# Index scores by pairs of heads on the two halves of TensorE's rows

## The chip, the cores and the metric

The kernel runs on one core of a Trainium2 chip. The metric is the time of one execution in microseconds (us) on the device; the kernel before took 3161.13 us in the median of three runs (3159.14 to 3167.12).

## What is computed

One layer of a streaming encoder: 2048 tokens of width 1024, float32. The part that the change touches is the indexer of a sparse attention. For each block of 128 queries, eight index heads of 64 dimensions score all admissible keys:

```
rel       = relu(einsum('bqhd,bsd->bqhs', q_idx, k_idx) * 64 ** -0.5)
idx_score = einsum('bqh,bqhs->bqs', w_idx * 8 ** -0.5, rel)
sel       = top_k(idx_score, 256)        # the keys that attention may use
```

Before and after it stand one wide input projection, a pooling mixer, gates, the attention over the selected keys, an output projection, a layer norm, a gated MLP with a short convolution, and a second layer norm.

## The kernel before, in words

Products keep float32 accuracy by splitting an operand into a high part that the engine's fast float32 format (F32R) holds exactly and a low rest. `mm3` makes three products: high by high, high by low, low by high.

Tokens go in 4 groups of 512 (`G`) or 16 blocks of 128. The index keys have 64 dimensions, half of the array's 128 rows. `keys` transposes them doubled and writes `kst`: rows 0 to 63 hold the high part, rows 64 to 127 the low part. In `index_scores`, `double` copies each head's 64 query columns twice, `prepare` transposes the eight doubled heads into a PSUM tile and splits it, so two products of 128 rows, query high and query low against `kst`, give all four partial products. ScalarE (ACT) then evicts the PSUM tile with a Relu and VectorE (DVE) multiplies by the head's weight and adds. Blocks 0 and 1 need no scores. A block of more than 1024 keys is done in two spans, each with a PSUM tile from the pool of two (`PS2`).

The scores and the selection after them are a background generator (`scores_and_selection`, for the groups 0 and 1, then 2, then 3). `select` finds each query's 256th largest score by 32 counting passes over the score tile's bits (threshold tile `F`), then for each block a scan, the mask, and its store to DRAM. The foreground is the projections and then attention. At each foreground step `turn` adds to a credit 0.75 (`RATE`) of the PE time that the planner's clocks (`Paced`) counted since the last, and takes background steps as long as the credit is positive and the planned backlog of DVE and ACT is under 3 us. A step is charged with its DVE or ACT work, whichever is larger. In attention, `load_mask(b)` runs the background to the end of block b if its selection is not yet there. The framework then lays out each engine's instructions in an order of its own, by when it expects inputs and buffers to be ready; an engine starts them in that order.

In the profile all operations have the line of the recording helper (L133), so tiles tell them apart: `kst` the index keys, `F` the thresholds, `msk` the masks in DRAM, `mx` the running minimum of an attention score row, `ident` the identity of transposes, `p` PSUM tiles, `b` and `m` tiles of the large and the middle pool (42 and 8 buffers).

Of the kernel before, what the change touches and what calls it, by code (L numbers as in the profile page):

```python
# [9 lines left out]
F32 = mybir.dt.float32  # L10
F32R = mybir.dt.float32r
# [3 lines left out]
AF = mybir.ActivationFunctionType  # L15
# [4 lines left out]
P = 128  # L20
# [30 lines left out]
NPRE = 2  # L51
PN = (1, 1, 1)
PG = (0,)
HD, HP = 3, 5
XAT = 0
SPC, SPN, SPG = 0, 1, 0
TLAG = 3
# [10 lines left out]
NFIRST = 1  # L68
FINE = "fine"
PAUSE = "pause"  # L70
GRAIN = 1
RATE = 0.75
CAP = 1.5
EARLY = 2
SWITCH = "A--"
# [24 lines left out]
class Paced:  # L100
# [5 lines left out]
    def __getattr__(self, name):  # L106
        f = getattr(self._e, name)
        if not callable(f) or name == "dma_start":
            return f

        def call(*args, **kw):
            out = args[0] if args else kw["out"]
            n = out.free_size()
            if self._w == "pe":
                self._c.pe += 0.109 if name == "transpose" else 0.002 + max(n, 64) / 2400.0
            else:
                rate = {"dve": 1.04, "act": 0.84, "pool": 2.2}[self._w]
# [228 lines left out]
class Kern:  # L346
# [83 lines left out]
    def turn(self, step=None):  # L430
        for t in self.late:
            t[0] -= 1
        while self.late and self.late[0][0] <= 0:
            self.late.pop(0)[1]()
        if step != FINE:
            for dst, src in self.older:
                self.nc.sync.dma_start(dst, src)
            self.older, self.stores = self.stores, []
        pe, work = self.clocks.pe, self.clocks.work
        self.credit = min(self.credit + RATE * (pe - self.seen), CAP)  # L440
        self.seen = pe
        while self.bg and self.clocks.backlog() < SLACK and self.credit > 0:
            ready, gen = self.bg[0]
            if not ready():
                break
            before = dict(work)
            step = next(gen, "end")
            if step == "end":
                self.bg.pop(0)
            if step == PAUSE:  # L450
                break
            self.credit -= max(work["dve"] - before["dve"], work["act"] - before["act"])

    def run_to_end(self, gen):
        for step in gen:
# [47 lines left out]
    def setup(self):  # L503
# [6 lines left out]
        self.kst = self.keys_pool.tile([P, S], F32R, tag="kst", name="kst")  # L510
# [254 lines left out]
    def keys(self, g, krs, kds):  # L765
# [8 lines left out]
        nc.scalar.dma_start(self.d_kT[g], kT)  # L774
        self.keyed = g
        ks = slice(g * G, (g + 1) * G)
        nc.scalar.activation(self.kst[0:64, ks], pi[0:64], AF.Copy)
        kh = self.M([P, G], F32R)
        nc.scalar.activation(kh[64:128], pi[64:128], AF.Copy)
        nc.vector.tensor_tensor(self.kst[64:128, ks], pi[64:128], kh[64:128].bitcast(F32), op=OP.subtract)  # L780

    def head_values(self, g, rows):

# [221 lines left out]


    def index_scores(self, g):
        nc = self.nc
        blocks = [b for b in range(g * RB, (g + 1) * RB) if b >= 2]
        rows, doubled, parts = {}, {}, {}  # L1010
# [18 lines left out]
        for _ in range(PN[0] if g in PG else 1):  # L1029
            yield PAUSE  # L1030
        double(blocks[0])
        for _ in range(PN[1] if g in PG else 1):
            yield PAUSE
        prepare(blocks[0])
        for _ in range(PN[2] if g in PG else 1):
# [1 line left out]
        for b in blocks:  # L1037
            N = P * (b + 1)
            more = b + 1 in blocks
            if more:  # L1040
                load(b + 1)
            qh, ql = parts.pop(b)
            if N <= 1024:
                spans = [(0, N)]
            else:
                spans = [(0, N - SPLIT[b // 2]), (N - SPLIT[b // 2], N)]
            tiles = [self.T([P, hi - lo]) for lo, hi in spans]
            self.I[b] = tiles
            for h in range(IH):
                if h == HD and more:  # L1050
                    double(b + 1)
                if h == HP and more:
                    prepare(b + 1)
                wsc = self.ws[:, b, h:h + 1]
                for t, (lo, hi) in enumerate(spans):
                    nch = 1 if hi - lo <= 512 else 2
                    cw = (hi - lo) // nch
                    ps = self.PS2([P, 2, 512])
                    for c in range(nch):
                        ks = slice(lo + c * cw, lo + c * cw + cw)  # L1060
                        nc.tensor.matmul(ps[:, c, :cw], qh[:, h], self.kst[:, ks], start=True, stop=False)
                        nc.tensor.matmul(ps[:, c, :cw], ql[:, h], self.kst[:, ks], start=False, stop=True)
                    rl = self.T([P, nch, cw])
                    nc.scalar.activation(rl, ps[:, :nch, :cw], AF.Relu, scale=ID ** -0.5)
                    rl = rl.rearrange("p c w -> p (c w)")
                    if h == 0:
                        nc.vector.tensor_scalar(tiles[t], rl, wsc, None, op0=OP.mult)
                    else:
                        nc.vector.scalar_tensor_tensor(tiles[t], rl, wsc, tiles[t], op0=OP.mult, op1=OP.add)
                    yield  # L1070
            w = tiles[-1].shape[1]
            getattr(nc, MS).memset(tiles[-1][0:64, w - 64:w], NEG)

    def select(self, halves):

# [1048 lines left out]
```

## Time and profile before

| | |
|---|---|
| median of three runs | 3161.13 us |
| the profiled execution | 3160.95 us, span 3159.2 us |
| granted TensorE clock, mean | 0.989 |
| busy: PE, DVE, ACT, POOL | 96, 77, 51, 17% |
| instructions | 43928 |

Busy time of PE counts pipelined matmuls with modelled ends, so their starts say more than their lengths. PEld are PE's weight loads, one before each product. A row that ends in `[7.63 <-DVE mx]` was idle for 7.63 us until DVE wrote `mx`.

### The profile page before, as it was taken

To read this page: it belongs to the slowest core of one execution; us is meant where nothing else is said; L and a number is where in the kernel's file an instruction comes from. 1 tells how busy PE (TensorE), PEld (TensorE's weight loads), DVE (VectorE), ACT (ScalarE), POOL (GpSimd) and SP (SyncE) were. 2 spreads that over 40 slices of the span, in tenths; PEclk is the share of its full clock that TensorE was granted. 3 is DMA by queue.
4 is the path that set the end of the run, shared out by engine and by line. 5 is a ranking of instruction groups with operands and counts; after the bars stand their busy time and mean duration, and the time that the engine had idled before them with its cause. 6 is when DMAs were issued, how large, how long until landed. Compare 5 with 4: busy or idle time off the path is not lost. (4 is left out here: it accounts for less than half of the span.)

```text
span 3159.2 us, 43928 instructions
## 1 busy us (share of the span) xinstructions
PE 3041.4 (96%) x14750; PEld 2536.1 (80%) x14750; DVE 2445.5 (77%) x4563; ACT 1613.7 (51%) x3085; POOL 541.5 (17%) x528
## 2 busy tenths in 40 slices
PE   8999899999999999979999999999999999999998
PEld 8887688888888788768787778887778888888887
DVE  5588887987699899888776688999886655656676
ACT  3468846874578787657611144444442222433253
POOL 2002010010020221100231234554411111100011
PEclk9999899999999999989999999999999999999999
DMA  7668783755466332221264778887888866998753
GB/s 255 242 208 298 262 336 138 275 213 184 145 256 250 102 104 84 70 80 62 82 225 162 262 259 303 299 296 284 289 305 321 313 214 224 366 397 328 262 199 110
DMA packets 325872, 715.88 MB, mean 227 GB/s; under 512 B 27466, under 2 KB 132366, under 8 KB 325646
## 3 DMA queue, kind: packets, MB, share of 16 engines
q1 hardware_dynamic: 317006, 697.34, 62.0%
q10 hardware_dynamic: 8640, 15.73, 1.3%
q8 instruction: 117, 1.92, 0.3%
q14 instruction: 109, 0.89, 0.1%
HBM read 454.85 MB, written 258.11 MB: 226 GB/s over the span
## 5 line engine op out<-in xcount | busy, mean ns | idle before, releaser
L133 PE MATMUL p<-b,b 128*128 128x512 f32 (+3 forms) x12568 | 2824.0, 381 | 71.3 <-DVE b L133 25.9
L133 PEld LDWEIGHTS p<-b,b 128*128 128x128 f32 x12568 | 2255.5, 190 | 511.0 <-DVE b L133 32.9
L133 DVE TENSOR_TENSOR b<-p,b 128x512 f32<-128x512 f32 (+3 forms) x622 | 390.6, 654 | 144.6 <-PE p L133 97.8
L133 ACT ACTIVATE b<-p 128x512 fp32r<-128x512 f32 (+11 forms) x634 | 360.6, 604 | 259.1 <-PE p L133 244.0
L133 ACT ACTIVATE b<-b 128x512 fp32r<-128x512 f32 (+3 forms) x344 | 270.5, 805 | 323.2 <-DVE b L133 143.4
L133 DVE TENSOR_TENSOR b<-b,b 128x1024 fp32r<-128x1024 f32 (+6 forms) x302 | 340.0, 1136 | 87.5 <-ACT b L133 38.0
L133 ACT ACTIVATE m<-b,F 128x448 bf16<-128x448 f32 (+3 forms) x448 | 366.2, 820 | 52.8 <-DVE F L133 40.3
L133 DVE TENSOR_SCALAR_CACHE_REDUCE m<-b,F 128x512 bf16<-128x512 f32 (+6 forms) x476 | 372.5, 808 | 7.3 <-DMA gm<-m 3.8
L133 ACT ACTIVATE b<-m 128x512 fp32r<-128x512 f32 x215 | 133.3, 628 | 345.0 <-DVE m L133 133.7
L133 DVE SCALAR_TENSOR_TENSOR b<-b,cw,b 128x1023 f32<-128x1023 f32 (+1 forms) x176 | 246.2, 1411 | 69.7 <-ACT b L133 68.7
L133 ACT ACTIVATE b<-b,cw 128x1024 f32<-128x1024 f32 x88 | 106.9, 1236 | 269.5 <-DVE b L133 260.5
L133 POOL TENSOR_TENSOR b<-b,b 128x1024 f32<-128x1024 f32 (+3 forms) x62 | 148.8, 2402 | 490.2 <-DVE b L133 289.4
L133 PE MATMUL p<-ident,b 128*128 128x128 f32 x1248 | 199.0, 278 | 17.0 <-DVE b L133 8.9
L133 ACT ACTIVATE b<-b,mx 128x1024 f32<-128x1024 f32 (+2 forms) x192 | 171.6, 896 | 70.5 <-DVE mx L133 68.1
L133 PEld LDWEIGHTS p<-ident,b 128*128 128x128 f32 x1248 | 154.3, 142 | 53.1 <-DVE b L133 13.1
L133 DVE TENSOR_TENSOR b<-m,b 128x512 fp32r<-128x512 f32 x215 | 155.6, 732 | 53.1 <-ACT b L133 52.9
L133 DVE SCALAR_TENSOR_TENSOR b<-b,ws,b 128x768 f32<-128x768 f32 (+5 forms) x154 | 154.0, 1025 | 42.2 <-ACT b L133 39.3
L133 DVE CUSTOM_DVE_ANT_0 b<-p,b 128x1024 f32<-128x1024 f32 (+7 forms) x128 | 125.6, 984 | 39.1 <-PE p L133 30.9
L133 PE MATMUL p<-kst,b 128*128 128x384 f32 (+3 forms) x656 | 147.8, 358 | 2.8 <-ACT b L133 2.0
L133 ACT ACTIVATE m<-p 128x512 f32<-128x512 f32 (+2 forms) x172 | 100.8, 586 | 74.6 <-PE p L133 67.9
L133 PEld LDWEIGHTS p<-kst,b 128*128 128x128 f32 x656 | 111.0, 188 | 23.1 <-ACT b L133 12.4
L133 DVE TENSOR_TENSOR b<-p,m 128x512 f32<-128x512 f32 x132 | 89.7, 682 | 10.8 <-PE p L133 10.7
(126 smaller groups left out, 1528.4 us busy)
## 6 DMA issues: line engine op xcount, KB each, us to landing
b<-wk SPq DMA_DIRECT2D x339, 512.0 KB
wk<-b SPq DMA_DIRECT2D x211, 512.0 KB
b<-h SPq DMA_DIRECT2D x88, 512.0 KB
b<-in_w_ffn_up_dram SPq DMA_DIRECT2D x44, 512.0 KB
h<-b SPq DMA_DIRECT2D x44, 512.0 KB
b<-vv SPq DMA_DIRECT2D x80, 256.0 KB
hs<-b SPq DMA_DIRECT2D x33, 512.0 KB
b<-hs SPq DMA_DIRECT2D x33, 512.0 KB
```

The costliest lines, as they stand in the source:

```text
L133: return f(*args, **kw)
```

## The change

The keys are kept in two tiles, `kih` (high parts) and `kil` (low parts, a tile of the large pool for each 1024 keys), each with the same 64 dimensions on rows 0 to 63 and again on rows 64 to 127. The queries are transposed in pairs, head 2j on rows 0 to 63 and 2j+1 on rows 64 to 127, four transposes a block, and are not doubled. For each pair three products of 64 rows per head are written alternately for the two heads: query high by key high, query high by key low, query low by key high. Both PSUM tiles of the pool belong to one pair. A span that crosses key 1024 has its middle product in two pieces. The planner counts a 64-row product at half, and a scoring step (`LIGHT`) is charged with 0.75/0.95 of its work.

```diff
-HD, HP = 3, 5
+HP = 2
+LIGHT = "light"
+INDEX_RATE = 0.95
 # Paced
-                self._c.pe += 0.109 if name == "transpose" else 0.002 + max(n, 64) / 2400.0
+                half = name == "matmul" and args[1].shape[0] == ID
+                self._c.pe += 0.109 if name == "transpose" else (0.002 + max(n, 64) / 2400.0) / (2 if half else 1)
 # turn
-            self.credit -= max(work["dve"] - before["dve"], work["act"] - before["act"])
+            spent = max(work["dve"] - before["dve"], work["act"] - before["act"])
+            self.credit -= spent * (RATE / INDEX_RATE if step == LIGHT else 1.0)
 # keys
-        nc.scalar.activation(self.kst[0:64, ks], pi[0:64], AF.Copy)
-        kh = self.M([P, G], F32R)
-        nc.scalar.activation(kh[64:128], pi[64:128], AF.Copy)
-        nc.vector.tensor_tensor(self.kst[64:128, ks], pi[64:128], kh[64:128].bitcast(F32), op=OP.subtract)
+        if g % 2 == 0:
+            self.kil.append(self.T([P, 2 * G], F32R))
+        nc.scalar.activation(self.kih[:, ks], pi, AF.Copy)
+        nc.vector.tensor_tensor(self.kil[-1][:, (g % 2) * G:(g % 2 + 1) * G], pi, self.kih[:, ks].bitcast(F32), op=OP.subtract)
 # index_scores
-        def double(b):
-            qd = doubled[b] = self.T([P, IH, 2, ID])
-            nc.vector.tensor_copy(qd, rows.pop(b).rearrange("p (h d) -> p h d", d=ID)[:, :, None, :]
-                                  .to_broadcast([P, IH, 2, ID]))
         def prepare(b):
-            qd = doubled.pop(b)
-            ps = self.PS2([P, IH, P])
-            for h in range(IH):
-                nc.tensor.transpose(ps[:, h], qd[:, h].rearrange("p a d -> p (a d)"), self.ident)
-            parts[b] = self.split_new(ps)
+            ps = self.PS2([P, IH // 2, P])
+            q = rows.pop(b)
+            for j in range(IH // 2):
+                nc.tensor.transpose(ps[:, j], q[:, j * P:(j + 1) * P], self.ident)
+            qs = parts[b] = self.T([P, 2, IH // 2, P], F32R)
+            self.split(qs[:, 0], qs[:, 1], ps)
...
-            for h in range(IH):
+            for j in range(IH // 2):
...
-                    ps = self.PS2([P, 2, 512])
+                    pss = [self.PS2([P, 2, 512]) for _ in range(2)]
...
-                        nc.tensor.matmul(ps[:, c, :cw], qh[:, h], self.kst[:, ks], start=True, stop=False)
-                        nc.tensor.matmul(ps[:, c, :cw], ql[:, h], self.kst[:, ks], start=False, stop=True)
+                        terms = [(0, self.kih, 0, k0, k1)]
+                        for i, kl in enumerate(self.kil):
+                            u, v = max(k0, 1024 * i), min(k1, 1024 * (i + 1))
+                            if u < v:
+                                terms.append((0, kl, 1024 * i, u, v))
+                        terms.append((1, self.kih, 0, k0, k1))
+                        for n, (i, k, o, u, v) in enumerate(terms):
+                            for e in range(2):
+                                r = slice(e * ID, (e + 1) * ID)
+                                nc.tensor.matmul(pss[e][:, c, u - k0:v - k0], qs[r, i, j], k[r, u - o:v - o],
+                                                 start=n == 0, stop=n + 1 == len(terms))
+                    for e in range(2):
+                        ps, pss[e] = pss[e], None
                         ...
-                    yield
+                        yield LIGHT
```

Where the instructions come to stand. First PE while the last group is scored, before (`kst`: index products; `p_3151` a projection of the foreground; 128x512 is the output tile):

```order
L133 MATMUL p_3143_10260<-kst,b_10150 128x512
L133 MATMUL p_3143_10260<-kst,b_10151 128x512
L133 MATMUL p_3143_10260<-kst,b_10150 128x512
L133 MATMUL p_3143_10260<-kst,b_10151 128x512
L133 MATMUL p_3145_10268<-kst,b_10150 128x512
L133 MATMUL p_3145_10268<-kst,b_10151 128x512
L133 MATMUL p_3145_10268<-kst,b_10150 128x512
L133 MATMUL p_3145_10268<-kst,b_10151 128x512
L133 MATMUL p_3151_10284<-b_7824,b_10012 128x512
```

Two heads' products, then foreground products; all use the whole array. Now, for one pair of heads of a later block (`kih` and `b_1335`, a `kil` tile: index products; `p_3029` is the PSUM tile of the head on rows 0 to 63, `p_3030` of the one on rows 64 to 127):

```order
L136 MATMUL p_3023_9954<-b_8413,b_9488 128x512
L136 MATMUL p_3029_9992<-kih,b_9696 128x448
L136 MATMUL p_3029_9992<-b_1335,b_9696 128x448
L136 MATMUL p_3029_9992<-kih,b_9696 128x448 x2
L136 MATMUL p_3030_9993<-kih,b_9696 128x448
L136 MATMUL p_3030_9993<-b_1335,b_9696 128x448
L136 MATMUL p_3030_9993<-kih,b_9696 128x448 x2
L136 MATMUL p_3029_9992<-b_1335,b_9696 128x448
L136 MATMUL p_3030_9993<-b_1335,b_9696 128x448
L136 MATMUL p_3029_9992<-kih,b_9696 128x448
L136 MATMUL p_3030_9993<-kih,b_9696 128x448
```

The pair's products do not alternate throughout: four of one head come first, then four of the other, and only the last four alternate.

Second, DVE at the end of the last selection, before (128x2048: block 15; `ISA` rows with `mx` are attention's scores with a mask; `b_16083` is the mask of block 14):

```order
L133 TENSOR_SCALAR b_16183<-b_16182 128x2048
L133 SCALAR_TENSOR_TENSOR b_16184<-b_16183 128x2048
L133 SCALAR_TENSOR_TENSOR nd_16189<-b_16184,fx_16094,cg_16093 128x1
L133 TENSOR_SCALAR nd_16189<-nd_16189 128x1
L133 TENSOR_SCALAR b_16183<-b_16184,nd_16189 128x2048
L133 TENSOR_TENSOR b_16182<-b_16182,b_16183 128x2048
L133 TENSOR_SCALAR b_16194<-b_16182 128x2048
L133 ISA b_16209,mx_16201<-p_4930_16202,b_16083 128x1024
```

The scan (the second row) and the rest of block 15's selection stand in one piece, right ahead of the score with block 14's mask. Now the scan of block 15 (second row) stands here, between foreground work,

```order
L136 TENSOR_SCALAR b_15988<-b_15987 128x2048
L136 SCALAR_TENSOR_TENSOR b_15989<-b_15988 128x2048
L136 TENSOR_TENSOR b_16078<-p_4797_16073,b_16078 128x512
L136 SCALAR_TENSOR_TENSOR nd_16070<-b_15989,fx_15300,cg_15299 128x1
L136 ISA b_16091,mx_16083<-p_4800_16084,b_14737 128x1024
```

and its mask (first row) here, ahead of the first score with block 12's mask (`b_16294`):

```order
L136 ISA mx_16297 128x1
L136 TENSOR_SCALAR b_16337<-b_15987 128x2048
L136 TENSOR_TENSOR b_16344<-p_4863_16339,b_16344 128x512
L136 TENSOR_TENSOR rinv_16349<-ssum_16141 128x4
L136 RECIPROCAL rinv_16349<-rinv_16349 128x4
L136 ISA b_16372,mx_16364<-p_4872_16365,b_16294 128x1024
```

Between the two pieces stand 39 rows, so the selection's end has moved ahead of all scores with masks 12 to 15.

## Rows read from the trace of the kernel before

**Rows 1.** The page's head: the span, then busy time of each engine, its share of the span and its instructions.
```profile
span 3159.2 us, 43928 instructions
...
PE 3041.4 (96%) x14750; PEld 2536.1 (80%) x14750; DVE 2445.5 (77%) x4563; ACT 1613.7 (51%) x3085; POOL 541.5 (17%) x528
```

**Rows 2.** Windows by stage, us from the span's start: length of the window, busy us (and instructions) of PE, PE's weight loads, DVE, ACT and POOL, the granted TensorE clock, the DMA share and GB/s.
```profile
750.00:880.00 130.00, 130.00 (x600) 107.80 (x600) 88.03 (x92) 70.59 (x84) 5.23 (x4) 1.00 0.44 155
...
1050.00:1290.00 240.00, 226.95 (x1333) 192.36 (x1332) 213.81 (x509) 188.56 (x421) 52.54 (x64) 0.99 0.32 97
1290.00:1400.00 110.00, 85.71 (x448) 71.13 (x447) 91.31 (x167) 63.87 (x125) 10.12 (x13) 0.88 0.24 79
```

**Rows 3.** Waits of PE between 1050 and 1400 us: total us, times, longest.
```profile
PE p L133 <- DVE mx L133: 24.0, 11, 7.6
PE p L133 <- DVE b L133: 7.7, 5, 3.1
```

**Rows 4.** Timeline of PE around the last masks: start us, length us of a run of like instructions, their number, and in brackets the idle time before and what ended it.
```profile
1350.11 2.19 PE L133 MATMUL p<-b,b 128*128 128x512 f32 x6 [4.16 <-DVE mx L133]
...
1357.77 0.66 PE L133 MATMUL p<-ident,b 128*128 128x128 f32 x4 [1.45 <-DVE m L133]
1366.06 5.82 PE L133 MATMUL p<-b,b 128*128 128x512 f32 x14 [7.63 <-DVE mx L133]
...
1380.97 2.93 PE L133 MATMUL p<-b,b 128*128 128x512 f32 x6 [7.06 <-DVE mx L133]
```

**Rows 5.** Timeline of DVE there: the scans that end the selection of blocks 14 and 15 (1920 and 2048 keys).
```profile
1357.64 4.14 DVE L133 TENSOR_TENSOR_SCAN b<-b 128x1920 f16<-128x1920 f16 x1
...
1372.13 4.42 DVE L133 TENSOR_TENSOR_SCAN b<-b 128x2048 f16<-128x2048 f16 x1
```

**Rows 6.** Timeline of SyncE's DMA issues there: a mask stored (`msk<-b`) and loaded (`b<-msk`).
```profile
1364.89 0.33 SPq L461 DMA_DIRECT2D msk<-b  x1
1367.46 0.32 SPq L1211 DMA_DIRECT2D b<-msk  x1
1379.80 0.32 SPq L461 DMA_DIRECT2D msk<-b  x1
1382.53 0.32 SPq L1211 DMA_DIRECT2D b<-msk  x1
```

**Rows 7.** The instructions that read the threshold tile `F`: counting passes of the selection on DVE; duration ns min/median/max, first and last start us.
```profile
L133 DVE TENSOR_SCALAR_CACHE_REDUCE m<-b,F x476: 332/868/1283, 186.0 to 1346.0; 128x128 bf16<-128x128 f32 x33, 128x320 bf16<-128x320 f32 x33, 128x768 bf16<-128x768 f32 x23, 128x640 bf16<-128x640 f32 x23
```

**Rows 8.** Timeline of PE while the last group is scored; the products with `kst` are the index scores.
```profile
802.77 1.77 PE L133 MATMUL p<-kst,b 128*128 128x448 f32 x8
804.38 1.55 PE L133 MATMUL p<-b,b 128*128 128x512 f32 x6
805.77 1.03 PE L133 MATMUL p<-ident,b 128*128 128x128 f32 x8
806.57 1.05 PE L133 MATMUL p<-kst,b 128*128 128x448 f32 x4
```

**Rows 9.** Instructions grouped by form: count, busy us, mean ns of one, and the engine's idle time before them: full products of 512 and 256 columns.
```profile
L133 PE MATMUL p<-b,b 128*128 128x512 f32 x10936 | 2598.1, 394 | 54.6 <-DVE b L133 24.4 <-DVE mx L133 21.4 <-ACT b L133 7.0
...
L133 PE MATMUL p<-b,b 128*128 128x256 f32 x928 | 132.3, 292 | 11.2 <-ACT b L133 8.7 <-DVE b L133 1.6 <-DVE mx L133 0.7
```

**Rows 10.** Timeline of PE where it turns to four transposes of 44 rows and back.
```profile
1819.68 1.52 PE L133 MATMUL p<-b,b 128*128 128x512 f32 x6
1821.13 0.44 PE L133 MATMUL p<-ident,m 44*128 44x44 f32 x4
1821.50 1.19 PE L133 MATMUL p<-b,b 128*128 128x512 f32 x4
```

**Rows 11.** The same at a transpose of 16 rows.
```profile
22.14 1.12 PE L133 MATMUL p<-b,b 128*128 128x256 f32 x8
23.19 0.23 PE L133 MATMUL p<-ident,m 16*128 16x16 f32 x1
23.35 0.62 PE L133 MATMUL p<-b,b 128*128 128x256 f32 x3
```

**Rows 12.** Timeline of PE's weight loads: four full loads.
```profile
1331.01 0.53 PEld L133 LDWEIGHTS p<-b,b 128*128 128x128 f32 x4
```

**Rows 13.** The weight loads of the index products: ns min/median/max.
```profile
L133 PEld LDWEIGHTS p<-kst,b x656: 186/188/193, 120.3 to 874.5; 128*128 128x128 f32 x164
```

**Rows 14.** Timeline of PE's weight loads: four loads of 44 rows.
```profile
1821.13 0.32 PEld L133 LDWEIGHTS p<-ident,m 44*128 44x128 f32 x4 [0.35 <-issue]
```

**Rows 15.** The loads of those small transposes: ns min/median/max.
```profile
L133 PEld LDWEIGHTS p<-ident,m x102: 132/141/230, 23.2 to 1821.3; 128*128 128x128 f32 x96, 44*128 44x128 f32 x4, 16*128 16x128 f32 x1, 4*128 4x128 f32 x1
```

**Rows 16.** Grouped by form: the doubling copies, the splits of the transposed index queries on DVE and ACT, the Relu of 896 columns.
```profile
L133 ACT ACTIVATE b<-p 128x896 f32<-128x896 f32 x40 | 35.9, 919 | 24.2 <-PE p L133 24.0
...
L133 DVE TENSOR_TENSOR b<-p,b 128x1024 fp32r<-128x1024 f32 x14 | 17.1, 1220 | 14.0 <-ACT b L133 14.0
...
L133 ACT ACTIVATE b<-p 128x1024 fp32r<-128x1024 f32 x14 | 14.5, 1032 | 9.1 <-PE p L133 8.3 <-DVE b L133 0.7
...
L133 DVE COPY b<-m 128x1024 f32<-128x1024 f32 x14 | 9.6, 687 | 2.8 <-DMA m<-qi 2.8
```

More of the change, by code (lines that the diff above doesn't have):

```diff
@@ L509, in setup @@
         self.ws = self.C([P, NB, IH], name="ws")
-        self.kst = self.keys_pool.tile([P, S], F32R, tag="kst", name="kst")
+        self.kih = self.keys_pool.tile([P, S], F32R, tag="kih", name="kih")
+        self.kil = []
         self.halo = self.C([P, 4, HALO], name="halo")
@@ L1009, in index_scores @@
         blocks = [b for b in range(g * RB, (g + 1) * RB) if b >= 2]
-        rows, doubled, parts = {}, {}, {}
+        rows, parts = {}, {}
         def load(b):
@@ L1014, in load @@
             nc.sync.dma_start(rows[b], self.d_qi[b])
-        def double(b):
-            qd = doubled[b] = self.T([P, IH, 2, ID])
-            nc.vector.tensor_copy(qd, rows.pop(b).rearrange("p (h d) -> p h d", d=ID)[:, :, None, :]
-                                  .to_broadcast([P, IH, 2, ID]))
         def prepare(b):
-            qd = doubled.pop(b)
-            ps = self.PS2([P, IH, P])
-            for h in range(IH):
-                nc.tensor.transpose(ps[:, h], qd[:, h].rearrange("p a d -> p (a d)"), self.ident)
-            parts[b] = self.split_new(ps)
+            ps = self.PS2([P, IH // 2, P])
[4 more added lines that the diff above has]
+            self.split(qs[:, 0], qs[:, 1], ps)
         load(blocks[0])
[L1029 to L1032, printed above, removed]
+        for _ in range(PN[0] + PN[1] if g in PG else 2):
             yield PAUSE
@@ L1041, in index_scores @@
                 load(b + 1)
-            qh, ql = parts.pop(b)
+            qs = parts.pop(b)
             if N <= 1024:
@@ L1048, in index_scores @@
             self.I[b] = tiles
-            for h in range(IH):
-                if h == HD and more:
-                    double(b + 1)
-                if h == HP and more:
+            for j in range(IH // 2):
+                if j == HP and more:
                     prepare(b + 1)
-                wsc = self.ws[:, b, h:h + 1]
                 for t, (lo, hi) in enumerate(spans):
+                    pss = [self.PS2([P, 2, 512]) for _ in range(2)]
                     nch = 1 if hi - lo <= 512 else 2
@@ L1057, in index_scores @@
                     cw = (hi - lo) // nch
-                    ps = self.PS2([P, 2, 512])
                     for c in range(nch):
-                        ks = slice(lo + c * cw, lo + c * cw + cw)
-                        nc.tensor.matmul(ps[:, c, :cw], qh[:, h], self.kst[:, ks], start=True, stop=False)
-                        nc.tensor.matmul(ps[:, c, :cw], ql[:, h], self.kst[:, ks], start=False, stop=True)
-                    rl = self.T([P, nch, cw])
-                    nc.scalar.activation(rl, ps[:, :nch, :cw], AF.Relu, scale=ID ** -0.5)
@@ L1065, in index_scores @@
[L1065 to L1069, printed above, removed]
-                    yield
+                        k0, k1 = lo + c * cw, lo + c * cw + cw
+                        terms = [(0, self.kih, 0, k0, k1)]
[3 more added lines that the diff above has]
+                                terms.append((0, kl, 1024 * i, u, v))
@@ new lines, in index_scores @@
+                        terms.append((1, self.kih, 0, k0, k1))
[6 more added lines that the diff above has]
+                        ps, pss[e] = pss[e], None
+                        wsc = self.ws[:, b, 2 * j + e:2 * j + e + 1]
+                        rl = self.T([P, nch, cw])
+                        nc.scalar.activation(rl, ps[:, :nch, :cw], AF.Relu, scale=ID ** -0.5)
+                        rl = rl.rearrange("p c w -> p (c w)")
+                        if j == 0 and e == 0:
+                            nc.vector.tensor_scalar(tiles[t], rl, wsc, None, op0=OP.mult)
+                        else:
+                            nc.vector.scalar_tensor_tensor(tiles[t], rl, wsc, tiles[t], op0=OP.mult, op1=OP.add)
+                        yield LIGHT
@@ L1071, in index_scores @@
             w = tiles[-1].shape[1]
             getattr(nc, MS).memset(tiles[-1][0:64, w - 64:w], NEG)
+        if g + 1 == NG:
+            self.kil = None
     def select(self, halves):
```

## The prediction

> **What bounds the kernel now.** Read the page's busy shares first: TensorE (PE) is busy for 3041.4 of 3159.2 us [rows 1], so almost every microsecond added to or taken from its stream shows in the time, unless a stage waits for something else. Then the windows by stage [rows 2]: while the last group of keys is scored (750 to 880 us) PE is busy 130.00 of 130.00 us, VectorE (DVE) only 88.03 and ScalarE (ACT) 70.59. The index scores are bound by PE there. The window 1290:1400 is different: PE 85.71 of 110 us, at a granted clock of 0.88. The waits of PE from 1050 to 1400 us name DVE's tile `mx`, the running minimum of attention scores, with 24.0 us [rows 3]. The timeline shows four long waits, 4.16, 1.45, 7.63 and 7.06 us [rows 4], and DVE, then the mask's stores, show why: the scans that end the selection of blocks 14 and 15 run at 1357.64 and 1372.13 [rows 5], each mask goes out only then and is read back 2.6 to 2.7 us later [rows 6], because attention asked for it. The selection is late: the last of its counting passes starts at 1346.0 us [rows 7].
>
> So two accounts decide: what the index products cost PE, and whether the late selection still stops it.
>
> **The products.** From 802.77 to 804.38 eight products with `kst`, 448 columns each, take 1.61 us [rows 8]: 0.201 us each, 0.449 ns a column. Blocks 2 to 15 have 128(b+1) keys, 17,024 columns together; eight heads and two products make 272,384 columns: 122.3 us. Now there are three products per head, 408,576 columns, but a product on 64 rows can run beside one on the other 64. Were all pairs side by side, 204,288 columns would be left, 91.7 us, a gain of 30.6. The new order of PE's instructions does not have that. It often puts three or four products of one head ahead of the other's (the other head's PSUM tile was not free when the order was laid out). I walked through all 1032 half products in it and let each run beside its neighbour only where that is of the other half and PE starts them in order: 766 passes where there were 656, 300,928 columns, 135.1 us. **Plus 12.8 us.** If the halves never overlap, 183.5 us, plus 61.2. I take the first: different rows, different PSUM tiles, nothing shared that a row names. Where a stretch opens with a pair, the second waits for its own load: at most 0.06 us in each of 93 stretches, 5.7 us; I take **plus 3**.
>
> **The changes of mode.** The 1032 half products stand in 93 stretches, with full-array products of the projections around each. Before, both kinds use the full array. What it costs to change, the trace shows in two places where PE turns to a transpose of fewer rows and back. Six 512-column products begin at 1819.68; one lasts 0.39 [rows 9], so they begin 0.226 apart, the last at 1820.81, and the next is due at 1821.04. The 44-row transposes begin at 1821.13 [rows 10], 0.09 late. They begin 0.07 apart, so a full product could follow the last (1821.34) at 1821.40; it comes at 1821.50, 0.10 late, and its four take 1.19 where 0.39 + 3 x 0.226 is 1.07, 0.12 more. Together 0.31 us. At 22.14 to 23.97 the same sum (256 columns, 0.29 long [rows 9] and 0.119 apart, a 16-row transpose between, counted as 0.06) gives 0.10 + 0.10 + 0.09 = 0.29 [rows 11]. 93 x 0.31 = **plus 29 us**. Below, only the un-hidden load of 0.06 each: 6 us; above, 0.40 each: 37.
>
> The loads of weights set no bound of their own. Four full loads begin within 0.53 us, each lasting 0.188: 0.113 apart [rows 12, 13]; four 44-row loads take 0.32, each lasting 0.14: 0.06 apart [rows 14, 15]. Two half loads (0.12) hide behind a half product of mean 396 columns (0.178). The Trainium skill says otherwise (TensorE: Matmul & The Clock Gate, section LDWEIGHTS): a load takes the time of its columns, and one of 32 rows as long as one of 128. By it each of the 266 pairs would take two full loads, 0.226 instead of 0.178, an estimate of 13 us more and a time of 3189; the trace's 0.06 against 0.113 disagrees, so I leave it out.
>
> **The transposes.** Eight per block become four: 56 fewer, at 0.100 us (eight from 805.77 to 806.57 [rows 8]): **minus 5.6 us**.
>
> PE's stream: 12.8 + 3 + 29 - 5.6 = **plus 39 us**, in stages where PE has no idle time.
>
> **The selection's tail.** A LIGHT step now costs 0.75/0.95 = 0.79 of its work against the credit, so the scores of a group end after fewer foreground products and the selection of blocks 12 to 15 begins earlier in the program. In the new order its counting passes stand before attention's first score; block 15's scan stands 48 rows, its mask row 4 rows, ahead of the first score with mask 12. Before, two of these scans stood between the scores that wait for them. So the four waits, 20.3 us, should go. With them goes the clock's loss: 14 products took 5.82 us where 0.39 + 13 x 0.226 = 3.33 is usual, six took 2.93 where 1.52 is [rows 4]: 3.9 us. **Minus 24 us**. At most all of the stage's idle 24.3 and 5 for the clock come back, 29; at least 10, since the ends of blocks 13 to 15 now load DVE in 1050:1290, where it is busy 213.81 of 240 [rows 2].
>
> **At nothing.** 14 copies on DVE go (9.6 us), and 14 splits shrink from 1024 to 512 columns (1.22 and 1.03 us each before) [rows 16]: cover for PE in the scoring stage, where DVE has 42 of 130 us free. Without that cover nothing is lost, since work is removed. The keys' split does its two steps on all 128 rows and drops one ACT step. Two big buffers of 42 are held until the last scores, against the doubled tile and half of the split tiles that go. The mask's DMAs and query loads keep number and size; the loads stand a step or two elsewhere on SP. The denser steps press DVE, but its work in that stage does not grow and PE's does.
>
> **Sum.** 39 - 24 = plus 15 on the profiled execution's 3160.95 us: **3176 us**; the median of the runs, 3161.13, is 0.2 us away. This case alone spans 3162 (0.25 us a stretch, no stagger, 29 back) to 3201 (0.40, 5.7 and 10).
>
> **Rivals.** *A, the halves do not run side by side.* 61.2 + 29 - 5.6 = 84.6, less 26 of tail (a slower PE gives the selection more time): 3220. For it: no row here has two products at once. Against: only the array's rows differ. The Trainium skill (same page, part 3) reports four 32-row products at 3.07 times the pace of one after another; no run here shows it yet.
>
> *B, faster: the changes of mode cost little.* The two places had a transpose that may have waited for its own input, which would be counted in my 0.31. At 0.06 each (the load alone) the sum is 12.8 + 0 + 6 - 5.6 - 29 = minus 16: 3145. With 24 back it is level at (24 + 5.6 - 15.8)/93 = 0.15 us a stretch; below 0.05 it is faster by over 0.3%. For it: the transposes needed inputs made elsewhere; against: both places agree within 0.02, before and after the small piece. The Trainium skill (TensorEngine Tiling, Key Properties) has a change of mode drain the array, which speaks against B; the 0.09 and 0.10 agree with it.
>
> *C, a new wait takes the tail's place.* Each pair holds both PSUM tiles of the two-buffer pool, so a step's first product waits for the eviction of the last one's: a Relu of 896 columns takes 0.919 [rows 16]. With 0.4 us in each of 88 pair steps, plus 35: 3211. For it: the order has heads apart just where the second tile was late. Against: the foreground stands between most steps, six products or 1.36 us, and `kst`'s products wait little now.
>
> **Chances.** Forecast 0.45, A 0.20, B 0.22, C 0.13. A measurement of this kernel tells about 0.3%, 9.5 us, from no change: 3151.6 to 3170.6. Faster: most of B, 0.19, and 0.03 of the forecast: 0.22. Same: 0.16 of the forecast, 0.03 of B, 0.04 of C: 0.23. Slower: the rest, 0.55. The range reaches into A and B, 3143 to 3222, with about 0.1 left above and 0.06 below.
>
> **What would show it.** Right: 1032 products with `kih` or a `kil` tile, half of them starting within 0.1 us of a partner; PE's next full product 0.2 us or more late after each stretch; the scoring stages longer by some 40 us together; no PE wait over 4 us on `mx` around the last masks and the clock at 1.00 there. Wrong, if partners start 0.2 us apart (A), if full products follow without delay (B), if PE waits for ACT before `kih` products (C), or if a wait of 20 us stands elsewhere before attention ends.

## The result, and the profile after

The changed kernel takes **3207.39 us**, the median of four runs (3198.69 to 3209.53), against 3160.51 us of the kernel before beside it: ratio 1.0141, 95% interval 1.0129 to 1.0154, 46.9 us slower. The profiled execution took 3207.32 us. The direction was forecast, but plus 15 was forecast: the size is wrong by a factor of three. Two executions lie far outside their series, 6149.61 us of the kernel before (beside e1 to e4) and 12265.56 of e9; the ratios leave them out, and the medians hardly feel them.

First the rows that answer to those of before. The page's head:

```profile
span 3205.5 us, 44505 instructions
...
PE 3090.3 (96%) x15070; PEld 2545.9 (79%) x15070; DVE 2436.7 (76%) x4549; ACT 1607.7 (50%) x3081; POOL 545.6 (17%) x528
```

PE is busy 48.9 us longer [rows 1], and its idle time is about as long as before. The first and the last window of [rows 2]:

```profile
750.00:880.00 130.00, 128.00 (x648) 96.17 (x647) 87.12 (x105) 60.70 (x79) 0.00 (x0) 1.00 0.38 134
...
1290.00:1400.00 110.00, 101.89 (x581) 85.31 (x580) 100.31 (x200) 78.26 (x165) 14.55 (x18) 0.97 0.23 68
```

PE still bounds the scoring stage, busy for 128.00 of 130 us. The stage around the last masks is better: PE busy 101.89 instead of 85.71 us, the clock 0.97 instead of 0.88. PE's waits from 1050 to 1400 us [rows 3] say why (total us, times, longest):

```profile
PE p L136 <- DVE b L136: 10.0, 7, 3.4
PE p L136 <- DVE mx L136: 9.9, 7, 3.9
```

The running minimum `mx` costs 9.9 us where it cost 24.0. Against the foreground the selection is earlier. The scans of blocks 14 and 15 on DVE's timeline [rows 5] come 36 us earlier and 16 us later than before, in a stretch where the foreground comes 45 to 79 us later:

```profile
1322.13 4.16 DVE L136 TENSOR_TENSOR_SCAN b<-b 128x1920 f16<-128x1920 f16 x1
...
1387.83 4.42 DVE L136 TENSOR_TENSOR_SCAN b<-b 128x2048 f16<-128x2048 f16 x1
```

The row of the counting passes [rows 7] has the last one start at 1297.6, not 1346.0 us:

```profile
L136 DVE TENSOR_SCALAR_CACHE_REDUCE m<-b,F x476: 275/832/1279, 126.8 to 1297.6; 128x128 bf16<-128x128 f32 x33, 128x320 bf16<-128x320 f32 x33, 128x768 bf16<-128x768 f32 x23, 128x640 bf16<-128x640 f32 x23
```

Then the index products, on PE's timeline (start us, length of a run of like instructions, their number), a pair of heads of 448 columns [rows 8]:

```profile
845.73 0.63 PE L136 MATMUL p<-b,b 128*128 128x512 f32 x2
846.29 0.46 PE L136 MATMUL p<-kih,b 64*128 64x448 f32 x1
846.60 0.36 PE L136 MATMUL p<-b,b 64*128 64x448 f32 x1
846.80 0.56 PE L136 MATMUL p<-kih,b 64*128 64x448 f32 x3
847.17 0.39 PE L136 MATMUL p<-b,b 64*128 64x448 f32 x2
847.38 0.56 PE L136 MATMUL p<-kih,b 64*128 64x448 f32 x3
847.78 0.36 PE L136 MATMUL p<-b,b 64*128 64x448 f32 x1
847.98 0.36 PE L136 MATMUL p<-kih,b 64*128 64x448 f32 x1
848.27 1.19 PE L136 MATMUL p<-b,b 128*128 128x512 f32 x4
```

In the program's order this visit has four products of one head, four of the other, four in turn. The last of these twelve begins at 847.98, 1.69 us after the first; one after another, 0.201 apart, they would need 2.2. So halves do run beside each other. But it is not the order that keeps them apart here. The pair whose order the change shows (`p_3029` and `p_3030`, by its place the 76th of 93 visits) has the same order, and its twelve products start two at a time, the last 1.13 us after the first:

```profile
840.40 0.48 PE L136 MATMUL p<-kih,b 64*128 64x448 f32 x2
840.72 0.37 PE L136 MATMUL p<-b,b 64*128 64x448 f32 x2
840.92 0.57 PE L136 MATMUL p<-kih,b 64*128 64x448 f32 x4
841.33 0.37 PE L136 MATMUL p<-b,b 64*128 64x448 f32 x2
841.53 0.37 PE L136 MATMUL p<-kih,b 64*128 64x448 f32 x2
```

PE starts the second head's first product 0.01 us after the first head's, though three products of the first head stand between them in the program. So it does not start the products of the two halves in program order, as the kernel's description and the prediction have it. What differs is when the second head's PSUM tile is free. ACT's timeline has the Relus of the pair before each of the two visits:

```profile
837.36 1.73 ACT L136 ACTIVATE b<-p 128x896 f32<-128x896 f32 x2 [1.43 <-PE p L136]
845.09 1.73 ACT L136 ACTIVATE b<-p 128x896 f32<-128x896 f32 x2 [1.43 <-PE p L136]
```

They end at 839.09, before the visit at 840.40, and at 846.82, within the visit at 846.29; there the second head's first product starts at 846.87. In the whole trace 73 visits hold products of both halves. The later half's first product comes 29.7 us after the earlier's in sum, and 21.4 us of that fall to 46 visits in which it starts 0.05 us after the end of a Relu.

The price of a visit stands at its ends. The two full products from 845.73 leave PE free at 846.18; the first half product comes at 846.29, 0.11 late. The second follows 0.31 later, not 0.20. The next full product comes 0.29 after the last half product, 0.09 late, and its four take 1.19 where 1.07 is usual. Together **0.43 us**, where the forecast had 0.31 and 0.03 for the stagger.

Where do the 46 us arise? I numbered the foreground's full products in order (12,616 in either trace) and subtracted the starts of before from those of the changed kernel. Number 4200, at the start of attention, comes 62.8 us late; one near the end, number 12,200, 46.1. So the scoring stages lose 63, not 39, and the rest gives back 17, not 24. The same difference for the experiments (us against the kernel before, one profiled execution each) is used below:

| full product (us in the kernel before) | 2100 (446) | 3150 (733) | 4200 (1034) | 12,200 (3054) |
|---|---|---|---|---|
| changed kernel | +19.7 | +46.2 | +62.8 | +46.1 |
| e5: full charge | +8.0 | +26.4 | +45.4 | +48.0 |
| e3: both heads in one tile | +7.8 | +16.6 | +17.3 | -2.8 |
| e6: e3 with full charge | -3.5 | +1.7 | +3.7 | +11.4 |
| e4: before, lower charge | +21.3 | +30.9 | +31.5 | +21.5 |
| e12: vv from POOL's queue | +14.4 | +38.9 | +55.3 | +34.8 |

### The profile page after: what moved, and what is told of

It reads as the page before. It is cut to its first block, busy times and chain, and to the rows that moved or that the text cites. A ratio compares the mean times of both kernels' runs of the same rounds, so it can differ in the third digit from the quotient of the medians.

```text
span 3205.5 us, 44505 instructions
## 1 busy us (share of the span) xinstructions
PE 3090.3 (96%) x15070; PEld 2545.9 (79%) x15070; DVE 2436.7 (76%) x4549; ACT 1607.7 (50%) x3081; POOL 545.6 (17%) x528
## 5 line engine op out<-in xcount | busy, mean ns | idle before, releaser
L136 PE MATMUL p<-b,b 128*128 128x512 f32 (+5 forms) x12944 | 2930.4, 381 | 56.9 <-DVE b L136 24.5
L136 PEld LDWEIGHTS p<-b,b 128*128 128x128 f32 (+1 forms) x12944 | 2313.0, 190 | 521.6 <-issue 35.0
L136 ACT ACTIVATE b<-p 128x512 fp32r<-128x512 f32 (+10 forms) x634 | 354.2, 593 | 323.3 <-PE p L136 311.4
L136 DVE TENSOR_TENSOR b<-p,b 128x512 fp32r<-128x512 f32 (+2 forms) x622 | 383.3, 642 | 149.9 <-PE p L136 100.9
L136 PE MATMUL p<-ident,b 128*128 128x128 f32 x1136 | 181.1, 276 | 10.8 <-DVE b L136 8.8
L136 PEld LDWEIGHTS p<-ident,b 128*128 128x128 f32 x1136 | 140.6, 142 | 42.7 <-DVE b L136 13.0
L136 PE MATMUL p<-kih,b 64*128 64x384 f32 (+3 forms) x656 | 163.1, 392 | 9.0 <-ACT b L136 6.7
L136 ACT ACTIVATE m<-p 128x512 f32<-128x512 f32 (+1 forms) x168 | 98.7, 588 | 82.5 <-PE p L136 72.8
L136 PEld LDWEIGHTS p<-kih,b 64*128 64x128 f32 x656 | 95.2, 193 | 44.9 <-ACT b L136 27.9
```

## Experiments

**The price of a visit: e1 and e2.** Two versions of the kernel before that differ only in the rows of an extra product (`0:64` in e1, `0:128` in e2):

```diff
+                    nc.tensor.matmul(ps[:, 0, :256], qh[0:64, h], self.kst[0:64, 0:256], start=True, stop=True)
                     for c in range(nch):
```

> The kernel before, with one extra product of 256 columns on rows 0 to 63 ahead of the index products of every head and span (176 in all); its result is overwritten by the next product. Theory (a change between 64-row and full products costs PE time of its own): 176 x (0.119 us for the product + 0.30 for going in and out: 0.095 late in, 0.09 late out, 0.11 for the load that the next full product can't hide) = +74 us against the kernel before. Rival (what looks like the price of a change is waiting for PSUM or inputs, as in rival B of the prediction): 176 x (0.119 + at most 0.06) = +21 to +32 us.

> The same extra products, on all 128 rows: the same order and number of products, no change of mode. Both theories: 176 x 0.119 = +21 us against the kernel before. The difference to the 64-row version is the price of 176 visits: 53 us by the theory (0.30 each), 0 to 11 by the rival.

Measured: e1 3244.85 us, 1.0273 (1.0252 to 1.0294), plus 85.1; e2 3178.33, 1.0057 (1.0041 to 1.0072), plus 18.6. PE's timeline in e1, two extra products and eight index products of 448 columns in one run, then foreground:

```profile
861.12 2.72 PE L133 MATMUL p<-kst,b 64*128 64x256 f32 x10
863.68 0.63 PE L133 MATMUL p<-b,b 128*128 128x512 f32 x2
```

The same run in e2:

```profile
801.45 2.01 PE L133 MATMUL p<-kst,b 128*128 128x256 f32 x10
803.30 1.07 PE L133 MATMUL p<-b,b 128*128 128x512 f32 x4
```

From the extra product to the next full one of the foreground it is 2.56 us in e1 and 1.85 in e2. The difference, 0.71 us, is two visits, without the late entry of the first. Over all 176 it is 66.5 us by the medians: **0.38 us a visit**; by product 4200 (98.5 against 25.1 late) 0.42, which is rather high, since the profiled execution of e1 is the slowest of its four. Compared visit by visit, the starts in the two traces differ by 0.39 in the median. The rival, at most 0.06, is out. The theory's 0.30 was too low again: the extra product comes 0.09 late and the second full product behind it 0.10, much as expected, but the first full one 0.19 and not 0.09. That fits two delays at each change, one of the product behind it and one of the next: here the second product after the way in is the first after the way out.

**The order and the tiles of the heads: e3.** One PSUM tile holds one chunk for both heads, so the order has them in turn and neither waits for a tile of its own:

```diff
-                    pss = [self.PS2([P, 2, 512]) for _ in range(2)]
                     for c in range(nch):
+                        ps = self.PS2([P, 2, 512])
...
-                                nc.tensor.matmul(pss[e][:, c, u - k0:v - k0], qs[r, i, j], ...
+                                nc.tensor.matmul(ps[:, e, u - k0:v - k0], qs[r, i, j], ...
+                        rl = self.T([P, 2, cw])
+                        nc.scalar.activation(rl, ps[:, :, :cw], AF.Relu, scale=ID ** -0.5)
```

> The changed kernel, with both heads of a pair in one PSUM tile (one chunk of up to 512 keys in each half of it), so that the order of PE's instructions can't have the heads apart: 1032 half products in 88 stretches, alternating throughout, 92.1 us of passes instead of 135.3. One Relu per chunk for both heads, two shorter DVE steps per chunk instead of one long per head. Theory (half of the loss in scoring is heads one after another, half the changes of mode at 0.40 us each): 43 us less than the changed kernel, 2 less for 5 stretches fewer, so about 3162 us, level with the kernel before; 3146 if the waits for evictions and the low clock of 100 to 250 and 550 to 650 us go too. Rival (loads bound a pair: two loads of 0.113 each, one after the other, so that alternating pairs of 396 columns take 0.226 instead of 0.178): 25 us dearer, 3187. Rival (PE waits for evictions in scoring whatever the order): 3190 or more.

Measured: 3158.92 us, 0.9997 (0.9987 to 1.0007), 48.5 us less than the changed kernel and level with the kernel before. The theory's size holds (45 forecast). How the gain divides between the order and the tiles was not tried, since both changed. PE's timeline:

```profile
508.64 0.42 PE L136 MATMUL p<-kih,b 64*128 64x320 f32 x2
508.90 0.39 PE L136 MATMUL p<-b,b 64*128 64x64 f32 x4
509.13 0.45 PE L136 MATMUL p<-kih,b 64*128 64x320 f32 x4
509.42 0.31 PE L136 MATMUL p<-b,b 64*128 64x320 f32 x2
509.56 0.30 PE L136 MATMUL p<-kih,b 64*128 64x320 f32 x2
```

Pairs start together, and pairs of 320 columns follow each other at 509.27, 509.42 and 509.56, 0.145 apart. Loads don't bound them, so the first rival is out; so is the second, which wanted 3190 or more. The account of product 4200 closes for the two runs with the full charge. e5 (below) has 131.3 us of passes where the kernel before has 122.0, 96 visits at 0.42 and 5.6 of transposes less: 9.3 + 40.3 - 5.6 = 44.0, and the product is 45.4 late. e6 (below) has 91.8 us of passes: -30.2 + 40.3 - 5.6 = +4.5, and it is 3.7 late.

**The charge: e4 to e7.** e4 is the kernel before with LIGHT for its scoring steps, e5 the changed kernel with

```diff
-INDEX_RATE = 0.95
+INDEX_RATE = 0.75
```

e6 is e3 with that line, and e7 the kernel before with `yield LIGHT` in `select` instead of in `index_scores`.

> The kernel before with the lower charge for scoring steps alone (0.75/0.95 of their work): products, tiles and queries as before, 111 stretches of scores instead of 120. Theory (the charge is what brings the selection forward and takes the tail's waits away): 17 to 24 us less than the kernel before, 3137 to 3144, with no wait of PE over 4 us on the running minimum around the last masks. Rival (denser scoring steps cost PE waits and clock in the scoring stages, some 18 us, which in the changed kernel look like a price of the pairs): 3155 to 3165, no gain.

> The changed kernel with the full charge for scoring steps again (the rate 0.75 in place of 0.95), pairs as they are: 96 stretches, 131.3 us of passes. Theory, now that the kernel before with the lower charge alone took 21 us more (31 more at the start of attention, 10 given back in it): denser scoring steps load DVE, the store of the values waits for DVE and holds SP's queue, the next weights come late, PE waits 8 us and its clock falls. Without them the changed kernel loses those 21 and 4 us of passes, but pays for 3 more stretches: 3184 us. Rival (the pairs themselves bring these waits, by their two PSUM tiles): no change in the scoring stages, and the tail's wait is back: 3217 to 3224.

> Both heads of a pair in one PSUM tile and the full charge for scoring steps: 96 stretches, 91.8 us of passes. Theory: what the full charge gives back in the kernel before (21 us) it gives here too, less 3 for eight more stretches: 3159 - 18 = 3141. Rival (the late weights came from the split of the chunks over more, shorter DVE steps, which stay): 3160, and with the tail's wait back up to 3175.

> The kernel before with the lower charge on the steps of the selection instead of those of the scores: 120 stretches, all products as before. Theory (the tail's waits go whenever the selection ends earlier, and scoring stages stay as they were): 10 to 20 us less than before, 3140 to 3150, PE's waits on the running minimum between 1050 and 1400 under 12 us instead of 24. Rival (a denser selection loads DVE in the projections and in attention, and delays stores and evictions there just as denser scores do): 3165 or more.

Measured: e4 3181.13, 1.0064 (1.0048 to 1.0080); e5 3208.89, 1.0150 (1.0133 to 1.0168); e6 3176.11, 1.0049 (1.0030 to 1.0067); e7 3180.38, 1.0063 (1.0043 to 1.0082). My theory fails in all four. e4 is slower by more than even its rival said, e5 is as slow as the changed kernel, which neither side had, and e6 and e7 stand with their rivals. The table and PE's waits from 1050 to 1450 us take two effects apart. In e4:

```profile
PE p L135 <- DVE mx L135: 5.2, 8, 1.7
```

In e5:

```profile
PE p L136 <- DVE mx L136: 29.1, 14, 9.8
```

With the lower charge the waits on `mx` are 5.2 us (e4), 10.6 (e3) and 9.9 (changed kernel), with the full one 29.1 (e5) and 32.5 (e6). So the charge does take the tail's waits away: from product 4200 to the end the changed kernel gains 16.7 us and e5 loses 2.6, **19.3 us**. But up to product 4200 the charge costs **17.4 us** with pairs (62.8 less 45.4; some 2.5 of it are 4 us of longer passes less three visits), 13.6 in e3 against e6, and 31.5 in the kernel before, whose products it doesn't touch. In the changed kernel gain and cost cancel. e7 shows that it isn't special to scores: with denser selection steps product 4200 is 61.1 late, the waits on `mx` are 6.0, and 42 us come back in attention.

**Where the charge costs: e8 to e11.** LIGHT only for some groups (g in (3,) or (2, 3)); e8 and e9 are e3 so changed, e10 is e9 with one step for both chunks of a span, e11 the kernel before with it:

```diff
-                        yield LIGHT
+                        yield LIGHT if g in (2, 3) else None
```

> Both heads of a pair in one PSUM tile, the lower charge only for the scores of the last group. Theory (by the delays of the foreground in the runs so far the lower charge costs 11 to 21 us in the groups 0 and 1, 4 to 10 in group 2, nothing in group 3, and what it gives in attention, 17 to 20 us, comes from the last selection's end): 3176 (full charge everywhere) - 20 - 3 for 8 visits fewer = 3153. Rival (the groups' scores and selections are one queue, so the last selection ends earlier only if those before it do): 3170 to 3176.

> The same with the lower charge for the scores of the groups 2 and 3, the full one for 0 and 1. Theory: the lower charge everywhere took 3159; of its cost 11 us lie in the groups 0 and 1, and its gain in attention stays: 3148. Rival (the gain needs the lower charge from the start): 3165 to 3176.

> The same, with one step of the background for both chunks of a span: 75 visits of 64-row products in place of 84. Theory (each visit costs 0.40 us): 3.6 us less than with a step per chunk, 3144. Rival (PE waits inside the longer visits for the Relu of the chunk before the last): 3150 or more.

> The kernel before (no pairs) with the lower charge for the scores of the groups 2 and 3 alone. Theory: of the 31 us that the lower charge cost it ahead of attention 21 lie in the groups 0 and 1 and go; 10 in group 2 stay; attention gives back 10 to 19: 3151 to 3160. If it lies at 3151, the pairs aren't what makes the faster version; if it stays over 3170, the delay doesn't hang on the group.

Measured: e8 3174.58, 1.0045 (1.0029 to 1.0061); e9 3158.72, 0.9990 (0.9981 to 1.0000); e10 3160.78, 0.9997 (0.9988 to 1.0007); e11 3153.76, **0.9977 (0.9968 to 0.9986)**. e8 stands with its rival: the waits on `mx` stay at 24.6 us. e9 falls between theory and rival: product 4200 is only 11.3 late, but attention gives back 10.0, where e3 got 20.1. e10's nine visits fewer bring nothing: product 4200 is 18.7 late, and where its longer steps lose that I didn't settle. e11, at 3151 to 3160 as expected, is with e15 the fastest on record, 0.23% under the kernel before, and has no pairs.

**How denser steps cost PE time: e12 to e15.** SyncE's timeline of DMA issues in the kernel before (`vv` the attention values, `xT` the transposed input, `in_w_in_dram` the next weights):

```profile
188.31 4.25 SPq L437 DMA_DIRECT2D vv<-b  x4
197.32 7.66 SPq L437 DMA_DIRECT2D qi<-b  x2
205.07 3.44 SPq L641 DMA_DIRECT2D b<-xT  x6
208.62 0.96 SPq L202 DMA_DIRECT2D b<-in_w_in_dram  x2
```

And after:

```profile
215.34 4.25 SPq L440 DMA_DIRECT2D vv<-b  x4
219.68 5.46 SPq L646 DMA_DIRECT2D b<-xT  x6
225.20 1.29 SPq L205 DMA_DIRECT2D b<-in_w_in_dram  x2
```

The weights are asked for at 225.20 instead of 208.62 us. SP's waits there, from 170 to 240 us, after:

```profile
SPq L440 <- DVE b L136: 43.0, 5, 40.0
```

ACT's timeline:

```profile
236.60 1.06 ACT L136 ACTIVATE b<-b 128x1024 fp32r<-128x1024 f32 x1 [11.61 <-issue]
```

PE's waits from 100 to 260 us:

```profile
PE p L136 <- ACT ws L136: 7.7, 1, 7.7
PE p L136 <- ACT b L136: 6.1, 8, 1.5
```

SP stands for 40.0 us (26.1 before) at a store of `vv` that DVE, pressed by the scores, has not made yet. Queued behind it are the loads of `xT` and of the weights; ACT splits the weights only at 236.60 (this row names no releaser; the next split waits for the weights' DMA), a small eviction to `ws` stands behind the split, and PE waits 7.7 us for it. e12 issues the `vv` stores from POOL, with PE's order unchanged:

```diff
-            self.store(self.d_vv[g][:, :, rb], t.rearrange("p h t e -> p h (t e)").bitcast(F32))
+            self.store(self.d_vv[g][:, :, rb], t.rearrange("p h t e -> p h (t e)").bitcast(F32), nc.gpsimd)
```

e13, e14 and e15 make the same move in the kernel before, in e3 and in e11.

> The changed kernel with one thing moved: the stores of the attention values (vv) are issued from POOL's queue instead of SP's; PE's order is the same. Theory (with the lower charge the store of vv waits 40 us for DVE at the head of SP's queue, so the next weights are asked for at 225 instead of 209 us, and PE waits 7.7 us for the ACT step behind them, with the clock at 0.90 after it): the weights are asked for before 212 us, that wait goes, and 8 to 13 us are saved: 3194 to 3199. Rival (SP would wait for something else there, DVE's queries or a free buffer, and the weights stay late): no change, 3204 to 3210.

> The kernel before with the stores of vv issued from POOL's queue, nothing else. Theory (only the denser scores make DVE late enough for these stores to hold back the next weights): no more than the 3.9 us that PE waits for an ACT step near 230 us, so 3156 to 3161. Rival (the stores hold SP in any version, and the gain has nothing to do with the change): 8 to 12 us less, 3148 to 3153.

> Both heads of a pair in one PSUM tile, lower charge everywhere, the stores of vv on POOL's queue. Theory (PE's wait there is 5.5 us, against 7.7 in the changed kernel, and the clock 0.93 against 0.90): 6 to 9 us less than without the move, 3150 to 3153. Rival (shorter DVE steps let the stores go anyway): 3157 to 3161.

> The kernel before (no pairs), the lower charge for the scores of the groups 2 and 3, the stores of vv on POOL's queue. Theory (the groups 0 and 1 go at the old pace, so there is little to win there): 0 to 4 us less than without the move, 3150 to 3154. Rival (the stores hold SP in any version): 3142 to 3146.

Measured: e12 3195.91, 1.0111 (1.0094 to 1.0128), 11.5 us less than the changed kernel, the time expected; e13 3161.12, 1.0003 (0.9994 to 1.0012), no gain; e14 3156.82, 0.9991 (0.9981 to 1.0000), 2 less than e3, where 6 to 9 were expected; e15 3153.98, 0.9979 (0.9970 to 0.9989), as e11. SP's issues in e12:

```profile
209.57 3.21 SPq L646 DMA_DIRECT2D b<-xT  x6
222.80 1.81 SPq L205 DMA_DIRECT2D b<-in_w_in_dram  x2
```

PE's wait:

```profile
PE p L136 <- ACT ws L136: 1.7, 1, 1.7
```

The wait on `ws` falls from 7.7 to 1.7 us, though the way there is not the one expected: `xT` is asked for 10 us earlier, the weights only 2.4, because SP now waits 34.7 us for PE, which frees a buffer for `xT`, and then 10.0 us for the store of `vv` to end. ACT splits the first weights at 228.72, 7.9 us earlier. Since the same move gives the kernel before nothing, the held queue belongs to the changed pace, and with e3's steps it costs little. At product 4200, 7.5 us of the 17.4 go with the move (62.8 to 55.3). The rest I can only locate, by the windows 100:250 and 550:650 (columns as in [rows 2]). Before:

```profile
100.00:250.00 150.00, 137.88 (x880) 123.83 (x879) 110.13 (x282) 94.86 (x201) 4.94 (x12) 0.99 0.65 217
550.00:650.00 100.00, 100.00 (x443) 82.66 (x442) 92.77 (x300) 82.20 (x181) 1.76 (x5) 1.00 0.79 279
```

After:

```profile
100.00:250.00 150.00, 133.20 (x834) 111.83 (x833) 89.70 (x234) 75.36 (x162) 1.66 (x4) 0.91 0.50 172
550.00:650.00 100.00, 93.35 (x434) 74.26 (x435) 83.12 (x225) 74.30 (x150) 0.00 (x0) 0.93 0.59 206
```

In e5:

```profile
100.00:250.00 150.00, 140.43 (x911) 116.89 (x910) 98.60 (x264) 85.00 (x186) 5.09 (x11) 0.98 0.61 204
550.00:650.00 100.00, 99.51 (x482) 79.90 (x481) 86.30 (x240) 75.72 (x156) 0.00 (x0) 1.00 0.65 228
```

The granted clock is 0.91 and 0.93 after, but 0.98 and 1.00 with the full charge. The other two pairs of runs that differ in the charge show the same. Up to product 4200 the traces' clock records have the clock at the lower of its two levels, 1.2 instead of 2.4 GHz, for this long, and PE is idle (the window less its busy time) for this long:

| to product 4200, us | low clock | PE idle |
|---|---|---|
| changed kernel (e5: full charge) | 54.6 (30.7) | 50.1 (46.0) |
| e3 (e6: full charge) | 41.0 (17.1) | 50.4 (43.6) |
| e4 (before: full charge) | 47.8 (20.5) | 58.4 (40.0) |

Half of the added time at the low clock and the added idle time make 16, 19 and 32 us, an estimate, beside the 17.4, 13.6 and 31.5 measured (in e3, eight visits fewer hide 3 more). So with pairs most of the charge's cost is the low clock. Ahead of the second loss PE waits 5.7 us for an ACT eviction, with counting passes ahead of it on ACT. What each of these waits costs by itself, and which of them brings the clock down, was not tried.

## Why the prediction was right in direction and wrong in size

- **Products, plus 12.8: right in size, partly by luck.** The halves run side by side, and what they lose is heads one after another: e3 brought 48.5 us where the walk through the order says 43.2 and five visits. But the walk let PE start the products in order, and at 840.40 it doesn't. In 46 of 73 visits the later head starts right behind the Relu on its PSUM tile. That the walk's sum came out fits the order having heads apart where that tile was expected late; this is argued and was not tried.
- **Changes of mode, plus 29, and stagger, plus 3: too small.** [rows 10] and [rows 11] gave 0.31 us with transposes of a few columns; a visit costs 0.38 to 0.43, since the second product after the way in is late too (by 0.11, not 0.03). 93 visits at 0.42 are 39, 7 more than the 32 forecast. The upper bound of 0.40 was the right size.
- **Loads, at nothing: right, by a wrong reading.** The 44-row loads 0.06 apart [rows 14] were taken for shorter loads. The loads of 128-row transposes last as long as theirs, 0.14 [rows 15], and a 64-row load lasts 0.184 where a full one lasts 0.188. They cost nothing because the two halves load at the same time.
- **Transposes, minus 5.6:** not measured by itself; the account closes with it.
- **At nothing, "the denser steps press DVE": this is the step that failed.** I counted DVE's work and PE's, but not what a later DVE holds back. Up to product 4200 the charge cost 17.4 us: PE waits, and 24 us more at the low clock than in e5. One path is shown: DVE later by some us holds a store on SP, which holds the next weights (e12, 7.5 us). For the rest the cause stays open.
- **Tail, minus 24: right in mechanism,** 19.3 by the charge; some of the waits of 24 moved to DVE's `b` (10.0 instead of 7.7) and some stayed on `mx`.
- **Sum as measured:** 12.8 + 39 - 5.6 + 17.4 - 19.3 = 44, beside 46.1 at product 12,200. The 2.5 us of products and visits in the 17.4 are counted twice here, so some 4 us stay unexplained.
- **Rivals.** A is out (e3). B is out (e1 against e2). C named PSUM evictions as the new wait, and its sign, PE waiting for ACT before `kih` products, did come. PE's waits for ACT's `b` in the three scoring stages (100:260, 430:640, 740:935) grow from 6.1 to 11.8 us together, 6 and not 35, but a head that waits while the other runs is in no such row: 21.4 us right behind a Relu. The walk had these counted as order, so C's 35 us on top of the forecast did not come: e5 closes without them.

Of the prediction's signs, "a wait of 20 us elsewhere" was looked for in one piece. It came as waits of 6 to 8 us and a lower clock. Of the signs for the forecast, 606 of the 1032 products start within 0.1 us of a partner, and no wait on `mx` around the last masks is over 3.9 us.

## What to carry to other kernels

Running two 64-row products side by side pays only if both can start together and a visit is long against its price, here 0.4 us: give both partners one PSUM tile, so that neither waits for a tile while the other runs alone. A change of pace in the background can have a price where the queues are: look for the instruction at the head of a DMA queue that waits for the engine you load, and for what stands behind it. And make a change of rates by itself before you put it down to the products that came with it.

## What the runs showed of the hardware

- Weights for the two halves of the rows don't queue behind each other as full loads do: pairs of 320 columns follow at 0.145 us, where two full loads need 0.226 [rows 12]. The Trainium skill (TensorE: Matmul & The Clock Gate, LDWEIGHTS) has a load of few rows take as long as a full one. The trace agrees on the length, 0.184 us against 0.188. Two such loads in turn would make it 0.226 a pair, an estimate from rows 12; e3's trace shows that they are not, since in the visit shown the loads of a pair start within 0.004 us of each other.
- Products of one half can start ahead of products of the other half that stand before them in the program: at 840.40 the second head's first product comes 0.01 us after the first head's, with three more of the first head's products between them in the order.
- After a change of mode, either way, two products are late, not one: the first by 0.09 to 0.11 us, and the second follows it after 0.31 instead of 0.20 us going in and comes 0.11 late on the way out. In the trace the second one's load begins 0.11 us after the first product, and not with it as between other products. The Trainium skill (TensorEngine Tiling, Key Properties) has a change of mode drain the array. The first delay at each end agrees with that, and the second is not in it.
